# Down projections of both FFNs in blocks of 1024 columns, with seven products for 7 of their 21 pairs of k-tiles

## The chip, the cores and the metric

The kernel runs on one core of one Trainium2 chip. The metric is device microseconds of one execution, median of a few. The core's engines are named as in the profile: PE (TensorE matmul), PEld (its weight loads), DVE (VectorE), ACT (ScalarE), POOL (GpSimd) and SP (SyncE, which issues the loads).

## The reference

One layer of a streaming encoder on 256 tokens of width 2048, all in float32: a half-step SwiGLU FFN, two parallel token mixers, cross-attention into 256 memory tokens and a second half-step FFN, each between a norm ahead and a norm behind, added to the residual x. The change lies in the two FFNs:

```
def swiglu(h, w_gate, w_up, w_down):
    return (jax.nn.silu(h @ w_gate) * (h @ w_up)) @ w_down
...
h = rmsnorm(x, n_ffn1_pre[l])
x = x + 0.5 * rmsnorm(swiglu(h, w_ffn1_gate[l], w_ffn1_up[l], w_ffn1_down[l]), n_ffn1_post[l])
```

D_FF is 5504, so that w_down is 5504 x 2048: 43 k-tiles of 128 rows by 2048 columns.

## The kernel before

Tokens lie in two tiles of 128. All weights are streamed once from HBM, most of them in raw tiles of 128 x 1024 float32 (512 KB). The host has laid them out so that each is one contiguous piece.

**A weight tile's way.** `weights` (L289 to L326) takes one of four raw buffers (`wraw`), loads it from SP's queue (L310), and splits it in two fp32r parts: ScalarE casts it to `whi` (L318), VectorE subtracts, `wlo = wraw - whi` (L319). `whi` and `wlo` hold three slots each. They are used in turn, and the counter `turn` goes on from one linear to the next. The raw buffer is free after the split, the slot when TensorE has multiplied with it.

**The product.** Every product is three matmuls: high part by high part, high by low, low by high. In the down projections (`lin_tok_steps`, L395 to L453; the matmuls are L410 to L412) tokens are stationary and 512 weight columns move, into one PSUM bank for each token tile. A raw tile holds two k-tiles of 512 columns, hence 12 matmuls (2 k-tiles, 2 token tiles, 3 parts). A column block c of 512 columns goes over all 43 k-tiles, and there are four of them. The gate and up projections have their matmuls in L374 and L378.

**An FFN** (`ffn`, L649 to L717) runs gate and up for 256 hidden columns at a time. The evacuations L655 to L668 make silu(gate) x up and split it to `mh` and `ml` (L501, L502; hidden k-tile by tokens), the stationary operands of the down projection. `post_norm` (L602 to L647) runs the four column blocks of the down projection. It squares each result for the norm (L496), multiplies it by the gain into `y` (L637), and in column block 3 makes the updates X += y x rstd (L620). The next norm's transposes are woven into column block 3 (`Passage`, L84 to L176). It also spills X to DRAM (`xsp`, L122) in the FFN ahead of the mixers.

**X**, the residual, is a tile of SBUF. In FFN1 it is loaded from the input in four DMAs of 512 KB during gate and up (L1644). It stays in SBUF through FFN2.

**Order.** Each engine has one instruction stream. A scheduler at build time orders the streams by priority: instructions as written, casts and splits 100 places earlier (`ahead`). A matmul sequence under `manual_schedule` keeps its order on PE. SP's loads stand in the order in which the raw tiles are made and wait for a free buffer.

## Time and profile before

| | |
|---|---|
| median of 3 executions | 2205.06 us (2204.56 to 2208.41) |
| the profiled execution's own time | 2203.17 us |
| its span, first to last instruction | 2201.4 us |
| PE / PEld / DVE / ACT / POOL busy | 2175.5 / 1943.7 / 1460.5 / 1140.5 / 105.8 us |
| mean granted clock of TensorE | 0.998 |
| HBM read and written | 436.51 MB, 10.49 MB |

Times inside an execution are read against the span: the profiled execution lasts 1.8 us longer than the span, and the median shown is 1.9 us above the profiled execution. FFN1's down projection lies at about 459 to 682 us of the span, FFN2's at about 1968 to 2190. In a row of the profile the name before "<-" is what is written and the names behind it are what is read. For a matmul, the name before the comma is the moving operand and the one behind it is the stationary operand.

### The profile page before, as it was taken

The numbers are of one execution on the slowest core, as the hardware profiler recorded it, in microseconds if no ns is written. First come the engines' busy times: TensorE is split into PE (matmuls) and PEld (weight loads), VectorE is DVE, ScalarE is ACT, GpSimd is POOL, SyncE is SP. The second block draws the span as 40 slices with busy tenths as digits, with TensorE's granted clock in tenths as the row PEclk, the third lists the DMA queues.
The fourth block names the chain that finished last, engine by engine and source line by source line (L and its number), as shares of the span: only waits on it lengthen the run. The fifth ranks groups of instructions, "written<-read, shape, count | busy, mean of one in ns | idle before, by whom it ended". The sixth has DMA issues, their size and how long they took to land.

```text
span 2201.4 us, 35059 instructions
## 1 busy us (share of the span) xinstructions
PE 2175.5 (99%) x13664; PEld 1943.7 (88%) x13664; DVE 1460.5 (66%) x2118; ACT 1140.5 (52%) x1706; POOL 105.8 (5%) x177
## 2 busy tenths in 40 slices
PE   9999999999999999999999999999999999999998
PEld 8999999988888889988778889988999999998887
DVE  7666666654457677778778766657766666664444
ACT  7555555544446555664444556446555555554443
POOL 0000000000000100101342000000000000000000
PEclk9999999999999999999999999999999999999999
DMA  7666666666666664555867765555666666666664
GB/s 262 221 210 200 201 201 202 201 213 206 208 210 209 219 209 148 186 173 191 253 201 249 272 206 193 172 176 177 201 201 201 201 201 201 201 209 206 209 204 157
DMA packets 130631, 449.30 MB, mean 204 GB/s; under 512 B 16161, under 2 KB 17697, under 8 KB 130209
## 3 DMA queue, kind: packets, MB, share of 16 engines
q1 hardware_dynamic: 122832, 429.84, 60.6%
q0 software_dynamic: 6768, 16.79, 2.5%
q8 instruction: 107, 1.75, 0.3%
q10 hardware_dynamic: 864, 0.44, 0.1%
q14 instruction: 60, 0.48, 0.1%
HBM read 436.51 MB, written 10.49 MB: 203 GB/s over the span
## 4 chain that ended last, share of the span: by engine, by line
PE 89%; DVE 6%; ACT 2%; issue 2%; DMA 1%; POOL 0%; DVEq 0%; ACTq 0%; POOLq 0%
PE mm L374 32%; PE mm L378 16%; PE mm L410 12%; PE mm L412 12%; PE mm L411 12%; DVE wlo L319 2%; ACT whi L318 1%; DVE tm L1214 0%; PE tr L514 0%; DMA wraw<-in_w_uq 0%; DVE X L620 0%; PE xo L1616 0%; DVE TT L1217 0%; DMA vsh<-vp 0%; PE xsc L1605 0%
## 5 line engine op out<-in xcount | busy, mean ns | idle before, releaser
L319 DVE TENSOR_TENSOR wlo<-wraw,whi 128x1024 fp32r<-128x1024 f32 (+3 forms) x792 | 954.3, 1207 | 618.5 <-ACT whi L318 606.2
L318 ACT CAST whi<-wraw 128x1024 fp32r<-128x1024 f32 (+3 forms) x792 | 818.4, 1034 | 785.3 <-PE mm L412 407.2
L374 PE MATMUL mm<-hT,whi 128*128 128x512 f32 x3280 | 1078.3, 384 | 0.6 <-ACT whi L318 0.6
L378 PE MATMUL mm<-hT,wlo 128*128 128x256 f32 x3280 | 879.9, 274 | 0.6 <-DVE wlo L319 0.6
L374 PEld LDWEIGHTS mm<-hT,whi 128*128 128x128 f32 x3280 | 614.0, 189 | 81.5 <-ACT whi L318 1.1
L378 PEld LDWEIGHTS mm<-hT,wlo 128*128 128x128 f32 x3280 | 630.0, 192 | 6.7 <-DVE wlo L319 1.0
L412 PE MATMUL mm<-whi,ml 128*128 128x512 f32 x680 | 257.8, 379 | 0.0
L410 PE MATMUL mm<-whi,mh 128*128 128x512 f32 x680 | 257.7, 379 | 0.0
L411 PE MATMUL mm<-wlo,mh 128*128 128x512 f32 x680 | 257.7, 379 | 0.0
L410 PE MATMUL mm<-whi,hT 128*128 128x512 f32 (+2 forms) x512 | 182.5, 357 | 0.9 <-DVE gt L1401 0.7
L411 PE MATMUL mm<-wlo,hT 128*128 128x512 f32 (+2 forms) x512 | 179.4, 350 | 1.7 <-DVE wlo L319 1.6
L412 PE MATMUL mm<-whi,hT 128*128 128x512 f32 (+2 forms) x512 | 178.3, 349 | 0.3 <-DVE hT L505 0.3
L411 PEld LDWEIGHTS mm<-wlo,mh 128*128 128x128 f32 x680 | 128.5, 189 | 18.3
L410 PEld LDWEIGHTS mm<-whi,mh 128*128 128x128 f32 x680 | 128.5, 189 | 18.2
L412 PEld LDWEIGHTS mm<-whi,ml 128*128 128x128 f32 x680 | 128.5, 189 | 18.2
L386 ACT COPY half<-mm 128x256 f32<-128x256 f32 x206 | 75.4, 367 | 115.4 <-PE mm L374 115.4
L387 DVE TENSOR_TENSOR half<-half,mm 128x256 f32<-128x256 f32 x206 | 86.0, 418 | 39.8 <-ACT half L386 39.7
L411 PEld LDWEIGHTS mm<-wlo,hT 128*128 128x128 f32 x512 | 97.2, 190 | 13.7 <-DVE wlo L319 4.9
L410 PEld LDWEIGHTS mm<-whi,hT 128*128 128x128 f32 x512 | 97.1, 190 | 12.6 <-DVE gt L1401 1.1
L412 PEld LDWEIGHTS mm<-whi,hT 128*128 128x128 f32 x512 | 97.1, 190 | 10.2 <-DVE hT L505 1.2
L469 POOL TENSOR_TENSOR rstd<-rstd,mhalf 128x1 f32<-128x1 f32 x22 | 15.2, 696 | 1697.7 <-DVE rstd L467 1697.7
L410 PE MATMUL mm<-whi,mT 128*128 128x512 f32 x128 | 48.7, 380 | 0.0
(312 smaller groups left out, 1760.6 us busy)
## 6 DMA issues: line engine op xcount, KB each, us to landing
wraw<-in_w_ffn_up SPq DMA_DIRECT2D x171, 512.0 KB, 3.8
wraw<-in_w_ffn_gate SPq DMA_DIRECT2D x170, 512.0 KB, 3.8
wraw<-in_w_ffn_down SPq DMA_DIRECT2D x168, 512.0 KB, 4.2
wraw<-in_w_in SPq DMA_DIRECT2D x124, 512.0 KB, 3.9
wraw<-in_w_o SPq DMA_DIRECT2D x32, 512.0 KB, 3.6
wraw<-in_w_ckv SPq DMA_DIRECT2D x32, 512.0 KB, 3.8
wraw<-in_w_oa SPq DMA_DIRECT2D x16, 512.0 KB, 3.5
wraw<-in_w_ob SPq DMA_DIRECT2D x16, 512.0 KB, 4.7
```

Source lines behind the costliest of these rows:

```text
L318: cast = self.last_cast = nc.scalar.copy(out=hi[:, e], in_=raw[:, e])
L319: self.last_split = nc.vector.tensor_sub(out=lo[:, e], in0=raw[:, e], in1=hi[:, e].bitcast(F32))
L374: both = lambda: nc.tensor.matmul(ps[j], hi[:, s], self.woven(x[:, k]), start=(k == 0), stop=(k == nk - 1))
L378: nc.tensor.matmul(ps[j][:, 0, :], lo[:, s], self.woven(x[:, k, 0]), start=False, stop=False)
L386: nc.scalar.copy(out=tokens, in_=low)
L387: nc.vector.tensor_add(tokens, tokens, high)
L410: nc.tensor.matmul(ps[t], part(xh, t, k), hi, start=(k == first), stop=False)
L411: nc.tensor.matmul(ps[t], part(xh, t, k), lo, start=False, stop=False)
L412: self.last_mm = nc.tensor.matmul(ps[t], part(xl, t, k), hi, start=False, stop=(k == last))
L469: nc.gpsimd.tensor_tensor(out=r, in0=r, in1=self.mhalf, op=ALU.pow)
```

## The change

The down projection is worked in two blocks of 1024 columns. Of its 43 k-tiles the first 30 are *wide*: a raw tile is one k-tile of 1024 columns. The other 13 are *narrow* as before. `_wide_order` gives the order of the 30: three single k-tiles, then seven times a pair of k-tiles and two singles (one behind the last pair).

A single is 2 token tiles x 2 column halves x 3 = 12 matmuls. A pair of k-tiles, two token tiles and two column halves are a product of 2 x 2 blocks by 2 x 2 blocks. Plainly this takes eight block products; by Strassen's scheme it takes seven, each of three matmuls. Products that belong to one result alone go into its own PSUM bank (`own`), where the singles add too, and the four others into four `shared` banks, over all seven pairs.

The sums of blocks that the scheme needs are made

- on the weight side by four in-place adds of 512 columns on VectorE per pair (L543 to L546), each sum then cast and split by `cut` (cast L510, split L511): w11 with 512 columns, w21|w22, e1|e3 and e4|e2 with 1024 each;
- on the token side by four sums per pair in the evacuation of gate and up (`left`, L488 to L491), kept with their splits in `S`;
- on the result side by `fix_wide` (L566 to L574), once per block: a ScalarE copy and eight VectorE additions on PSUM, with a scratch tile `part` that takes one of the four raw buffers.

`cut` uses six slots: the three of `whi` and `wlo`, and three in `room`, the space of the tile `hT` that is free then. It starts with the first slot in each block. The narrow k-tiles use the ring of three as before (L335 is now the load and L344 the split there). Those of the block's second half begin (k-tiles 30 to 35), then `fix_wide` is issued, then the first half is finished (30 to 42) and evacuated, then the second (36 to 42).

To make room, `y` is kept in two halves, `S` and X share a place, and X is loaded only behind the narrow tiles of column block 2: four DMAs of 512 KB, from the input in FFN1 and from `xsp` in FFN2. The cross-attention writes X to `xsp` for that, eight DMAs of 256 KB. The host lays w_down out in the new order.

```diff
+SPAIRS = range(2, 9)
+WIDE, EARLY = 30, 36
+def _wide_order():
+    rest = [k for k in range(WIDE) if k // 2 not in SPAIRS]
+    out, rest = rest[:3], rest[3:]
+    for i in SPAIRS:
+        out.append((2 * i, 2 * i + 1))
+        out, rest = out + rest[:2], rest[2:]
+    assert not rest
+    return out
...
+    def left(self, g0, g1, mh, ml, k, sh, sl):
+        nc = self.nc
+        d = self.tmp.tile([P, 512], F32, tag="junk", name="sums").rearrange("p (a t) -> p a t", a=4)
+        nc.vector.tensor_sub(d[:, 0], g0[:, P:], g1[:, P:])
+        nc.vector.tensor_sub(d[:, 1], d[:, 0], g0[:, :P])
+        nc.vector.tensor_sub(d[:, 2], g0[:, :P], g0[:, P:])
+        nc.vector.tensor_add(d[:, 3], g1[:, :P], d[:, 1])
+        self.split(g1, mh[:, k + 1, :], ml[:, k + 1, :])
+        self.split(d[:, 0], mh[:, k, P:], ml[:, k, P:])
+        self.split(d[:, 1:], sh, sl)
...
+    def lin_wide(self, w, b, mh, ml, sums, ring, banks):
+        nc = self.nc
+        own, shared = banks
+        seen, turn = set(), [0]
+        last = _wide_order()[-1]
+        def cut(raw):
+            n = raw.shape[-1]
+            hi, lo = (x[:, :n] for x in ring[turn[0] % len(ring)])
+            turn[0] += 1
+            with self.ahead(self.lead):
+                self.last_cast = nc.scalar.copy(out=hi, in_=raw)
+                self.last_split = nc.vector.tensor_sub(out=lo, in0=raw, in1=hi.bitcast(F32))
+            return [(self.paired(hi[:, i : i + 512]), self.paired(lo[:, i : i + 512])) for i in range(0, n, 512)]
+        def product(bank, x, wt, stop=False):
+            (xh, xl), (hi, lo) = x, wt
+            start = id(bank) not in seen
+            seen.add(id(bank))
+            nc.tensor.matmul(bank, xh, hi, start=start, stop=False)
+            nc.tensor.matmul(bank, xh, lo, start=False, stop=False)
+            nc.tensor.matmul(bank, xl, hi, start=False, stop=stop)
+        def load():
+            raw = self.wraw.tile([P, WT], F32, tag="wraw", name="wraw")
+            o = P * WT * (b * KF + self.wide_at)
+            nc.sync.dma_start(out=raw, in_=w[o : o + P * WT].rearrange("(p x) -> p x", p=P))
+            self.wide_at += 1
+            return raw
+        at = lambda k, t: tuple(x[:, k, t * P : (t + 1) * P] for x in (mh, ml))
+        self.wide_at = 0
+        for item in _wide_order():
+            if isinstance(item, int):
+                halves = cut(load())
+                for t in range(NT):
+                    for h in range(2):
+                        product(own[t][h], at(item, t), halves[h], item == last)
+                continue
+            k0, k1 = item
+            ra, rb = load(), load()
+            a0, a1, b0, b1 = ra[:, :512], ra[:, 512:], rb[:, :512], rb[:, 512:]
+            (w11,), (w21, w22) = cut(a0), cut(rb)
+            with self.ahead(self.lead):
+                nc.vector.tensor_add(a0, a0, a1)
+                nc.vector.tensor_add(a1, a1, b1)
+                nc.vector.tensor_add(b1, a0, b1)
+                nc.vector.tensor_add(b0, b1, b0)
+            (e1, e3), (e4, e2) = cut(ra), cut(rb)
+            s2, s3, s4 = sums(k0 // 2 - SPAIRS[0])
+            end = k0 // 2 == SPAIRS[-1]
+            product(shared[0], at(k0, 0), w11, end)
+            product(own[0][0], at(k1, 0), w21)
+            product(own[0][1], s4, w22)
+            product(shared[1], at(k0, 1), e1, end)
+            product(shared[2], s3, e3, end)
+            product(shared[3], s2, e2, end)
+            product(own[1][0], at(k1, 1), e4)
+    def fix_wide(self, banks, part):
+        nc = self.nc
+        own, (p1, p5, p7, p6) = banks
+        u, v = part[:, :512], part[:, 512:]
+        add, sub = nc.vector.tensor_add, nc.vector.tensor_sub
+        with self.ahead(3 * self.lead):
+            nc.scalar.copy(out=u, in_=p1)
+            add(own[0][0], own[0][0], u)
+            add(u, p6, u)
+            sub(v, p5, u)
+            add(u, p7, u)
+            add(own[1][0], own[1][0], u)
+            add(own[0][1], own[0][1], v)
+            sub(v, v, p7)
+            add(own[1][1], own[1][1], v)
...
+            room = self.hpool.tile([P, KD * 2 * T], F32R, tag="hT", name="room", bufs=1)
+            slots = [(x[:, a : a + WT], z[:, d : d + WT]) for x, z, d0 in (
+                (self.whi, self.wlo, 0), (room, room, RING * SLOT)) for a in range(0, RING * SLOT, SLOT) for d in (a + d0,)]
+            banks = {}
+            def narrow(c, ks, ev, *args):
+                base = c // 2 * KF * P * WT + (WIDE * WT + c % 2 * (KF - WIDE) * 512) * P
+                self.lin_tok(
+                    wd, KF, 0, 512, mh, ml, ev, *args, 0, [banks[c // 2][0][t][c % 2] for t in range(NT)],
+                    (ks, lambda k: base + (k - WIDE) * P * 512))
+            def lin(c, ev, passage):
+                b = c // 2
+                if c % 2:
+                    narrow(c, range(EARLY, KF, 2), ev, (7 if passage else SKEW) * (c == 3), passage)
+                    return
+                make = lambda pool, tag: [pool.tile([P, 512], F32, tag=tag, name="mm") for _ in range(2)]
+                one = [make(self.pst, "tr"), make(self.pss, "sm")]
+                two = [make(self.psm, "mm"), make(self.psm, "mm")]
+                own, shared = (two, one) if b else (one, two)
+                banks[b] = [list(x) for x in zip(*own)], [x for p in shared for x in p]
+                with self.tc.manual_schedule(engines={mybir.EngineType.PE}):
+                    self.lin_wide(wd, b, mh, ml, lambda n: [(x[:, 0], x[:, 1]) for x in (sums(n)[:, i] for i in range(3))],
+                                  slots, banks[b])
+                    narrow(c + 1, range(WIDE, EARLY, 2), None, 0, None)
+                    self.fix_wide(banks[b], self.wraw.tile([P, WT], F32, tag="wraw", name="part"))
+                    narrow(c, range(WIDE, KF, 2), ev, 0, None)
+                if b:
+                    self.X = self.hpool.tile([P, NT, D], F32, tag="big", bufs=1, name="X")
+                    for i in range(4):
+                        t, s = i // 2, slice(i % 2 * 1024, (i % 2 + 1) * 1024)
+                        self.after(nc.sync.dma_start(
+                            out=self.X[:, t, s], in_=residual[t * P : (t + 1) * P, s]), self.last_split)
+            return self.post_norm(lin, post, True, *after)
...
-        self.X = self.hpool.tile([P, NT, D], F32, tag="big", name="X")
...
-                    if c0 <= 256 * 5:
-                        feed[1](c0 // 256 - 2)
...
-                a["n_x_post"], False, "n_ffn2_pre")
+                a["n_x_post"], False, "n_ffn2_pre", None, xsp)
```

PE, FFN1's first pair behind the three singles (`mm` is any PSUM bank; `room` and `whi`, `wlo` are slots of weights; `S` holds token sums). The last four of its seven products:

```order
L518 MATMUL mm<-room,mh 128x512
L519 MATMUL mm<-room,mh 128x512
L520 MATMUL mm<-room,ml 128x512
L518 MATMUL mm<-room,S 128x512
L519 MATMUL mm<-room,S 128x512
L520 MATMUL mm<-room,S 128x512
L518 MATMUL mm<-whi,S 128x512
L519 MATMUL mm<-wlo,S 128x512
L520 MATMUL mm<-whi,S 128x512
L518 MATMUL mm<-whi,mh 128x512
L519 MATMUL mm<-wlo,mh 128x512
L520 MATMUL mm<-whi,ml 128x512
```

A pair is 21 rows of this kind; two k-tiles by 1024 columns were 24 rows of L410 to L412.

DVE, inside FFN1's down projection. Before, a column block's tiles follow each other:

```order
L319 TENSOR_TENSOR wlo<-wraw,whi 128x1024 x17
L319 TENSOR_TENSOR wlo<-wraw,whi 128x512
L319 TENSOR_TENSOR wlo<-wraw,whi 128x1024 x2
L637 TENSOR_TENSOR y<-mm,g 128x512
L319 TENSOR_TENSOR wlo<-wraw,whi 128x1024
L637 TENSOR_TENSOR y<-mm,g 128x512
```

Of the change, the last group of block 0 and its end, where the narrow tiles (L344) begin:

```order
L511 TENSOR_TENSOR room<-wraw,room 128x512
L543 TENSOR_TENSOR wraw<-wraw 128x512
L544 TENSOR_TENSOR wraw<-wraw 128x512
L511 TENSOR_TENSOR room<-wraw,room 128x1024 x2
L545 TENSOR_TENSOR wraw<-wraw 128x512
L546 TENSOR_TENSOR wraw<-wraw 128x512
L511 TENSOR_TENSOR wlo<-wraw,whi 128x1024 x2
L344 TENSOR_TENSOR wlo<-wraw,whi 128x1024
L567 TENSOR_TENSOR mm<-mm,part 128x512
L344 TENSOR_TENSOR wlo<-wraw,whi 128x1024
L568 TENSOR_TENSOR part<-mm,part 128x512
L569 TENSOR_TENSOR part<-mm,part 128x512
```

Between the splits stand the sums of a pair, and between the first narrow splits the corrections. The first split of a narrow tile stands ahead of the first correction.

SP, the end of FFN1's down projection and the start of the next linear. Before:

```order
L310 DMA wraw<-in_w_ffn_down 128x1024 x14
L310 DMA wraw<-in_w_ffn_down 128x512
L310 DMA wraw<-in_w_in 128x1024 x5
L122 DMA xsp<-X 128x512 x2
```

And now:

```order
L335 DMA wraw<-in_w_ffn_down 128x1024 x3
L335 DMA wraw<-in_w_ffn_down 128x512
L877 DMA X<-in_x 128x1024 x4
L335 DMA wraw<-in_w_in 128x1024 x4
L148 DMA xsp<-X 128x512
```

The four loads of X stand behind the last tile of w_down and ahead of the first of w_in; they stood among the loads of gate and up before.

More of the change, by code (lines that the diff above doesn't have):

```diff
@@ L402, in lin_tok_steps @@
             self.extra = {extra: passage.slots[0], extra + 2: passage.slots[1]}
-        ps = [self.psm.tile([P, n], F32, tag="mm", name="mm") for _ in range(NT)]
+        begun = ps is not None
+        if not begun:
+            ps = [self.psm.tile([P, n], F32, tag="mm", name="mm") for _ in range(NT)]
         def part(x, t, k):
@@ L409, in step @@
             hi, lo = self.paired(hi), self.paired(lo)
-            nc.tensor.matmul(ps[t], part(xh, t, k), hi, start=(k == first), stop=False)
-            nc.tensor.matmul(ps[t], part(xh, t, k), lo, start=False, stop=False)
-            self.last_mm = nc.tensor.matmul(ps[t], part(xl, t, k), hi, start=False, stop=(k == last))
+            more = {"skip_group_check": True} if begun else {}
+            nc.tensor.matmul(ps[t], part(xh, t, k), hi, start=(k == first and not begun), stop=False, **more)
+            nc.tensor.matmul(ps[t], part(xh, t, k), lo, start=False, stop=False, **more)
+            self.last_mm = nc.tensor.matmul(ps[t], part(xl, t, k), hi, start=False, stop=(k == last), **more)
         held = []
-        for k, hi, lo in self.weights(w, nk, c0, n):
+        for k, hi, lo in self.weights(w, nk, c0, n, at=at):
             if k < before:
@@ L668, in ev_up @@
                     nc.vector.tensor_mul(gate[j], ps, gate[j])
-                    self.split(gate[j], mh[:, k, :], ml[:, k, :])
+                    if k // 2 not in SPAIRS:
+                        self.split(gate[j], mh[:, k, :], ml[:, k, :])
+                    elif j == 0:
+                        self.split(gate[j][:, :P], mh[:, k, :P], ml[:, k, :P])
+                    else:
+                        v = sums(k // 2 - SPAIRS[0])
+                        self.left(gate[0], gate[1], mh, ml, k - 1, v[:, :, 0], v[:, :, 1])
                 return ev_gate, ev_up
```

101 lines of the change are left out of this document (60 added, 41 removed).

## The prediction

> **What bounds the kernel now.** I read the busy times and the chain of waits first, then the sums of the two stretches in which the down projections run, then single rows there.
>
> ```profile
> span 2201.4 us, 35059 instructions
> PE 2175.5 (99%) x13664; PEld 1943.7 (88%) x13664; DVE 1460.5 (66%) x2118; ACT 1140.5 (52%) x1706; POOL 105.8 (5%) x177
> PE 89%; DVE 6%; ACT 2%; issue 2%; DMA 1%; POOL 0%; DVEq 0%; ACTq 0%; POOLq 0%
> ...
> 460.00:682.00 222.00, 222.00 (x1031) 194.28 (x1031) 112.18 (x106) 95.10 (x106) 0.55 (x1) 1.00 0.67 210
> 1968.00:2190.00 222.00, 222.00 (x1030) 194.43 (x1029) 108.59 (x103) 92.88 (x102) 0.55 (x1) 1.00 0.64 196
> ```
>
> The last two rows are windows (length; then busy time and instructions of PE, PEld, DVE, ACT and POOL; granted clock; DMA share; GB/s). In both, TensorE is busy from end to end at clock 1.00, VectorE half of the time. TensorE alone sets the time there, so removing matmuls pays in full as long as what feeds it keeps up. 222.00 / 1031 = 0.2153 us is the distance of two matmuls; the busy time of one (below) is longer because matmuls overlap. The same from single rows of the timeline (start, duration):
>
> ```profile
> 588.04 0.38 PE L412 MATMUL mm<-whi,ml 128*128 128x512 f32 x1
> 588.68 0.38 PE L412 MATMUL mm<-whi,ml 128*128 128x512 f32 x1
> 589.10 1.05 ACT L318 CAST whi<-wraw 128x1024 fp32r<-128x1024 f32 x1 [1.54 <-PE mm L412]
> 590.18 1.23 DVE L319 TENSOR_TENSOR wlo<-wraw,whi 128x1024 fp32r<-128x1024 f32 x1 [1.37 <-ACT whi L318]
> 591.69 1.05 ACT L318 CAST whi<-wraw 128x1024 fp32r<-128x1024 f32 x1 [1.54 <-PE mm L412]
> 593.22 0.38 PE L412 MATMUL mm<-whi,ml 128*128 128x512 f32 x1
> ```
>
> The first and the last PE row are 24 matmuls apart: (593.22 - 588.04) / 24 = 0.2158 us, which I use. A tile of 12 matmuls takes 2.59 us, the distance of the casts. A cast waits for TensorE to leave its slot: it starts 0.04 us behind the end of the slot's last matmul (588.68 + 0.38), 0.2 after the next matmul's turn. The split starts 0.03 us after the cast's end. Both are done long before the tile is used, as the three slots run ahead.
>
> **What is saved.** A pair of k-tiles by seven products of three matmuls takes 21 matmuls where it took 24. 7 pairs x 2 blocks x 2 FFNs = 28 pairs save 84 matmuls, and 84 x 0.2158 = **18.1 us**. The busy time of a row is the wrong price:
>
> ```profile
> L412 PE MATMUL mm<-whi,ml 128*128 128x512 f32 x680 | 257.8, 379 | 0.0
> ```
>
> 84 x 0.379 would be 31.8 us, but the 379 ns of neighbours overlap.
>
> **What VectorE and ScalarE get for it.** A steady group is now a pair and two single k-tiles: 21 + 24 = 45 matmuls, 9.71 us of TensorE. Prices of the new work:
>
> ```profile
> L319 DVE TENSOR_TENSOR wlo<-wraw,whi 128x1024 fp32r<-128x1024 f32 x761 | 931.4, 1225 | 612.3 <-ACT whi L318 600.1 <-PE xpt L1610 0.5
> L318 ACT CAST whi<-wraw 128x1024 fp32r<-128x1024 f32 x761 | 797.6, 1048 | 776.3 <-PE mm L412 402.9 <-PE mm L374 164.2 <-issue 118.4
> L319 DVE TENSOR_TENSOR wlo<-wraw,whi 128x512 fp32r<-128x512 f32 x11 | 7.5, 685 | 1.0 <-ACT whi L318 1.0
> L318 ACT CAST whi<-wraw 128x512 fp32r<-128x512 f32 x11 | 6.7, 617 | 1.8 <-PE mm L412 1.7
> L1541 DVE TENSOR_TENSOR t<-t,ya 128x512 f32<-128x512 f32 x8 | 5.5, 686 | 0.0
> L637 DVE TENSOR_TENSOR y<-mm,g 128x512 f32<-128x512 f32 x32 | 21.9, 684 | 1.4 <-ACT junk L496 1.4
> ...
> 665.62 1.22 DVE L319 TENSOR_TENSOR hT<-wraw,hT 128x1024 fp32r<-128x1024 f32 x1 [0.39 <-ACT hT L318]
> 666.76 1.22 DVE L319 TENSOR_TENSOR wlo<-wraw,whi 128x1024 fp32r<-128x1024 f32 x1
> ```
>
> Two splits that follow each other start 1.14 us apart, 0.08 less than the duration; so a 512-column add is 0.61 behind unrelated work and 0.69 + 0.03 = 0.72 where it needs the one before. VectorE per group: five splits of 1024 (w21|w22, e1|e3, e4|e2, two singles) 5.70, the 512 one 0.61, four adds about 2.6, together 8.9 us of 9.71, or 92%, where it had 50%. ScalarE: 5 x 1.05 + 0.62 = 5.9. Neither is over the 9.71, so throughput costs nothing; what remains is latency through the buffers.
>
> **The loop through the buffers.** Four raw buffers, four loads of 512 KB per group. Loads already wait for a buffer:
>
> ```profile
> SPq L310 <- DVE wlo L319: 1205.2, 533, 6.9
> wraw<-in_w_ffn_down SPq DMA_DIRECT2D x168, 512.0 KB, 4.2
> ...
> wraw<-in_w_ffn_down SPq DMA_DIRECT2D x13, 512.0 KB, 3.4
> ...
> wraw<-in_w_in SPq DMA_DIRECT2D x1, 512.0 KB, 3.5
> ...
> wraw<-in_w_ob SPq DMA_DIRECT2D x16, 512.0 KB, 4.7
> ```
>
> (Issue to landing, KB and us: the page's median of 4.2; a stretch at 472 to 508 us with 3.4; one load at 914 that came alone behind another, 3.5; the slowest group, 4.7.) In the new order the second raw tile of a pair goes into the buffer that the group's first single leaves, and this single's split stands behind the pair's work on VectorE. Around that loop: load L; hand-over 0.03; cast w21|w22 1.05; 0.03; its split 1.14; split e1|e3 1.14; adds L545 and L546 0.72 + 0.61; the single's split 1.23; 0.03: L + 5.98 us. Against 9.71 it binds if L is over 3.7. I take L = 3.5: no other load is issued in the 2.5 us ahead of it and few bytes are in flight (the 3.4 and 3.5 rows). Then 9.5 < 9.71 and the loop costs 0. At 4.2 each group is 0.5 us late, six groups on end per block less the lead of 2 us, about 1.7 per block, 7 us in four blocks; at 4.7, 4 x (6 x 1.0 - 2) = 16 us.
>
> The Trainium skill, "DMA: Bandwidth & Descriptors", section "Anatomy of one DMA", gives for another issuing path 2.0 us plus the bytes at 436 GB/s, by estimate 3.2 us for this tile. By that the loop would be 9.2 us and the sum the same; no row here shows 512 KB under 3.4, so the rule is the kinder end.
>
> **Where slots clash.** The wide block always begins at slot 0 of its six and ends with k-tile 29 in slot 1, while the ring of three of the other linears goes on from where it stood. Followed through the tables: FFN1's block 0 and FFN2's block 1 begin when slot 0 still holds the tile TensorE has just multiplied. The first cast can then start only behind that tile's last matmul: 0.2 + 1.05 + 0.03 + 1.23 - 0.2 (one matmul needs no split) = 2.3 us of idle TensorE that nothing covers, twice, **4.7 us**. In the same two blocks k-tile 30 wants slot 1, which k-tile 29 still holds: 2.4 each, since its split can stand behind a correcting add; FFN1's block 1 half a microsecond, FFN2's block 0 nothing: **5.3 us**. If loads take 4.2 us these last become 3.7, 3.7 and 3.0, together 10.4. The bounds: nothing, if each cast finds a free slot; and load, cast and split in a row (3.5 + 1.05 + 1.23, some 6 us) at both ends of the four blocks, 46 us. I take the value near the low end, as only the clashes named have no free slot, and the raw tiles are there.
>
> **The rest.** Eight corrections per block on VectorE (L567 to L574, 0.69 each by the two add rows, 5.5 us, behind one ScalarE copy) are issued beside three narrow tiles, 7.8 us of TensorE; with the three splits VectorE has 8.9 us there, 1.1 too many, and makes it up in the ten narrow tiles behind, where it has 1.14 us of work per 2.59: 0. Uncovered they would cost 4 x 5.5 = 22 us. For the first group of the two blocks that begin without a clash I put 0.6 together. The sums on the token side (L488 to L491 and the smaller splits) lie in the column blocks of gate and up, some 21 us each:
>
> ```profile
> 453.89 0.42 DVE L502 TENSOR_TENSOR ml<-sg,mh 128x256 fp32r<-128x256 f32 x1
> ...
> 420.00:441.50 21.50, 21.50 (x133) 19.78 (x132) 14.90 (x22) 11.21 (x17) 0.00 (x0) 1.00 0.61 197
> ```
>
> Splits of 1024, 512 and 256 take 1.22, 0.69 and 0.42, so 128 columns about 0.29 and 384 about 0.55: two splits of 256 (0.84) become one of 256, two of 128, one of 384 and four sums of 128, 2.7 us, 1.9 more. VectorE goes from 14.9 to 16.8 of 21.5, 78%, hidden by the three slots of lead: 0. Without that cover it would be 14 pairs x 1.9 = 27 us. X late: four DMAs of 512 KB queue on SP ahead of the first tiles of the next stage in FFN1 (and ahead of the last w_down tiles in FFN2). X is needed only by the first update in column block 3, some 11 us after issue, and four transfers at 210 GB/s last 10: 0 to 1.6 in FFN2, I put 0.5. The eight spills of 256 KB in the cross-attention lie on a queue whose windows leave a third of the DMA time: 0 to 1. Without cover, 2 MB at 210 GB/s is 10 us each.
>
> **Sum.** -18.1 + 0 (loop) + 4.7 + 5.3 + 0.6 + 0.5 + 0.4 (spill) = -6.6 us against the profiled execution of 2203.2 us (span 2201.4 and 1.8 around it), 2196.6. The median shown is 2205.06, 1.9 above the profiled one; on its scale **2198.5 us**.
>
> **Rivals.**
> 1. *The loading loop decides, slower.* If w_down tiles land in 4.2 us, the page's median, the loop is 10.2 > 9.71: -18.1 + 7 + 4.7 + 10.4 + 1.5 = +5.5, 2210.6; at 4.7 some +14, 2219. It decides from L = 3.7 and turns the sign near 3.9. For: the median row. Against: the 3.4 and 3.5 rows at a like distance of issues, and that 216 GB/s (2 MB per 9.71 us) is hardly above the 210 of today.
> 2. *It ends level.* L between 3.7 and 4.0 costs 2 to 5 us in the loop and 2 more at the hand-overs: 2201 to 2207. For: nothing in the rows parts 3.5 from 3.9 in a new rhythm.
> 3. *The change gives its full 18.* If the slots are free in time or the clash costs only a cast, the loss is under 3 us: 2187 to 2190. Against: cast and split are in order on engines whose rows show no shorter form.
> 4. *The clock falls in the new gaps.* A TensorE that waits 3.7 us (rival 1's hand-overs) could be granted a lower clock behind it: at half speed for as long again it loses 1.8 us, with three such gaps 5.5, so 2216. For and against: no row above holds a gap of this size, so the profile of before cannot say. The Trainium skill, "TensorE: Matmul & The Clock Gate", section "What's actually happening", has the clock fall to half after an idle window of about 3.4 us; by it the gaps of my forecast, 2.4 us, change nothing, and those of rival 1 may. The row of the windows, 1.00 throughout, bears on neither.
>
> **How the numbers follow.** About 0.2%, 4.4 us, can be told from no change: same is 2200.6 to 2209.5. Forecast 0.45 with its own range 2192 to 2203 (0.36 of it faster, 0.09 same); rival 1 0.24 (0.20 slower, 0.04 same); rival 2 0.18 (0.15 same, 0.02 slower, 0.01 faster); rival 3 0.10, faster; rival 4 0.03, slower. Faster 0.47, same 0.28, slower 0.25. The range runs from 2190, which leaves out most of rival 3, to 2214, which leaves out the far end of rival 1 and rival 4.
>
> **What would show it.** TensorE with 84 fewer matmuls at the same 0.216 us, and in the two wide stretches PE idle only at block starts (about 2.3, cast and split named as releasers, L518 and L519) and at k-tile 30 (L410, L411). If rival 1 is right, each group shows an idle of L518 or L519 on `room` tiles, behind a cast that waited for a DMA, and w_down loads of 4 us or more. If rival 3 is right, no gap over 1 us stands there. An idle PE in gate and up, or at L620's X, would mean that covers I counted as whole are not. I am wrong altogether if VectorE, at 92% of a group, is what TensorE waits for without any load being late.

## The result: slower by 1.2%

| | before | changed |
|---|---|---|
| median | 2205.51 us (2204.56 to 2208.41, 4 runs) | 2232.9 us (2226.64 to 2234.2, 4 runs) |
| ratio | | 1.0116, 95% interval 1.0095 to 1.0138 |
| profiled execution, span | 2203.17 us, 2201.4 us | 2234.20 us, 2232.4 us |

The forecast was 2198.5 us, in a range from 2190 to 2214. The time lies outside it, and the sign is wrong. The two spans by stage (windows of the trace: length; then busy time and instructions of PE, PEld, DVE, ACT and POOL; granted clock; DMA share; GB/s), first before, then the changed kernel. The stages are gate and up of FFN1, its down projection, everything up to FFN2's down projection, and that:

```profile
0.00:459.40 459.40, 457.21 (x2774) 419.81 (x2775) 320.48 (x459) 249.88 (x374) 2.79 (x9) 1.00 0.66 212
459.40:682.70 223.30, 223.30 (x1038) 195.39 (x1037) 112.85 (x109) 95.91 (x108) 0.55 (x1) 1.00 0.67 211
682.70:1967.90 1285.20, 1272.04 (x8823) 1133.60 (x8822) 912.10 (x1442) 700.43 (x1120) 99.15 (x164) 1.00 0.62 202
1967.90:2190.80 222.90, 222.90 (x1033) 194.88 (x1031) 109.49 (x104) 92.88 (x102) 0.55 (x1) 1.00 0.63 195
```

```profile
0.00:460.10 460.10, 456.50 (x2774) 418.11 (x2774) 331.35 (x501) 253.68 (x388) 2.80 (x9) 1.00 0.64 208
460.10:696.60 236.50, 223.84 (x994) 189.76 (x994) 180.69 (x204) 116.43 (x136) 0.55 (x1) 0.98 0.61 203
696.60:1987.40 1290.80, 1274.22 (x8824) 1133.22 (x8823) 924.45 (x1488) 704.99 (x1135) 99.60 (x164) 1.00 0.63 203
1987.40:2222.00 234.60, 222.21 (x991) 188.81 (x989) 179.06 (x204) 114.08 (x132) 0.55 (x1) 0.98 0.59 195
```

The down projections have 42 matmuls fewer each and yet last 13.2 and 11.7 us longer: 24.9 of the 31.0 us between the spans. TensorE idles in them for 12.7 and 12.4 us, where it was busy throughout, and its granted clock is 0.98 instead of 1.00. The stage between is 5.6 us longer, gate and up 0.7.

**What TensorE waited for** (engine and line, what ended the wait; us in all, times, longest; the whole execution), before and now:

```profile
PE mm L411 <- DVE wlo L319: 2.2, 4, 0.9
```

```profile
PE mm L439 <- DVE wlo L344: 11.2, 13, 2.3
PE mm L519 <- DVE wlo L511: 9.1, 18, 1.0
PE mm L518 <- ACT whi L510: 5.0, 4, 3.4
PE mm L438 <- ACT whi L343: 3.9, 4, 1.1
```

L519 is the wait inside the pairs, mostly for e4|e2's split, 18 times up to 1 us. L518 is mostly the block starts. L438 is the step to the narrow tiles, and so are 6.3 us of L439; its other 4.9 lie in the stage between, where L411 had the 2.2 before. The rows of the step in FFN1's block 0:

```profile
539.68 0.38 PE L520 MATMUL mm<-whi,ml 128*128 128x512 f32 x1
541.19 0.48 PE L438 MATMUL mm<-whi,mh 128*128 128x512 f32 x1 [1.13 <-ACT whi L343]
543.92 0.48 PE L439 MATMUL mm<-wlo,mh 128*128 128x512 f32 x1 [2.24 <-DVE wlo L344]
544.24 0.50 PE L440 MATMUL mm<-whi,ml 128*128 128x512 f32 x1
544.53 0.63 PE L438 MATMUL mm<-whi,mh 128*128 128x512 f32 x1
544.96 0.63 PE L439 MATMUL mm<-wlo,mh 128*128 128x512 f32 x1
```

Between 539.68 and 543.92 lie 3.8 us more than two matmuls' distance. From 544.5 on matmuls follow each other at 0.43 us instead of 0.216, until 547.9. The granted clock of that stretch, and of the one behind it, in windows:

```profile
543.90:547.90 4.00, 3.98 (x11) 3.17 (x12) 1.27 (x2) 0.00 (x0) 0.00 (x0) 0.57 0.49 157
548.50:552.50 4.00, 4.00 (x20) 3.50 (x19) 1.77 (x2) 1.88 (x2) 0.00 (x0) 1.00 0.17 54
```

Eleven matmuls in 4 us at clock 0.57, then twenty at 1.00. This half clock comes behind five gaps of this execution. From the starts of consecutive matmuls, each distance over 0.3 us less 0.216 (and the run of 0.43 us distances likewise), the two down projections lose:

| | forecast | measured |
|---|---|---|
| matmuls saved | -18.1 | -18.1 |
| block starts (FFN1 block 0, FFN2 block 1) | 4.7 | 2.4 + 4.6 = 7.0 |
| step to the narrow tiles (three blocks) | 5.3 | 3.8 + 3.1 + 3.9 = 10.8 |
| inside the pairs, four blocks | 0 | 2.7 + 5.2 + 4.8 + 1.8 = 14.5 |
| half clock behind the five gaps | 0 | 1.7 + 1.7 + 1.7 + 1.7 + 2.7 = 9.5 |
| others (forecast: first groups of two blocks; measured: last tiles of FFN2) | 0.6 | 1.3 |
| down projections, sum | -7.5 | +25.0 |

**The loads.** The four loads of a group in FFN1's block 0 (timeline of SP's queue; then the DMA view of 501 to 522 us, two groups: GB/s in 40 equal slices, and the median from issue to landing; last, what the casts into `room` waited for in the whole execution):

```profile
501.66 4.55 SPq L525 DMA_DIRECT2D wraw<-in_w_ffn_down  x4
...
GB/s 0 0 0 133 320 406 180 164 211 304 297 304 304 281 351 351 273 117 0 0 0 0 0 148 328 406 187 117 179 367 281 289 296 265 297 390 304 117 8 31
...
wraw<-in_w_ffn_down SPq DMA_DIRECT2D x8, 512.0 KB, 4.7
...
ACT room L510 <- DMA wraw<-in_w_ffn_down: 71.9, 49, 3.3
```

All four are issued within 4.6 us, then none for 6, and for the five slices of 0 nothing moves. By place in the group, a block's means are 3.7 to 4.1 us for the pair's first tile, 4.3 to 4.7 for its second, 4.8 to 5.1 for the singles.

### The profile page after: what moved, and what is told of

Read it like the earlier page. It is cut to its first block, busy times and chain, and to the rows that moved or that the text cites. A ratio compares the mean times of both kernels' runs of the same rounds, so it can differ in the third digit from the quotient of the medians.

```text
span 2232.4 us, 35351 instructions
## 1 busy us (share of the span) xinstructions
PE 2176.8 (98%) x13580; PEld 1929.9 (86%) x13580; DVE 1621.1 (73%) x2402; ACT 1190.6 (53%) x1794; POOL 106.2 (5%) x177
## 4 chain that ended last, share of the span: by engine, by line
PE 68%; DVE 11%; DMA 9%; issue 7%; ACT 4%; POOL 1%; SPq 0%; ACTq 0%; DVEq 0%; POOLq 0%
PE mm L399 30%; PE mm L403 15%; DMA wraw<-in_w_ffn_down 7%; PE mm L439 6%; PE mm L438 6%; PE mm L440 6%; DVE wlo L344 3%; DVE room L511 3%; ACT whi L343 2%; DVE wlo L511 1%; ACT room L510 1%; DVE wraw L545 1%; PE mm L519 1%; PE mm L520 1%; DMA squares<-in_xT 1%
## 5 line engine op out<-in xcount | busy, mean ns | idle before, releaser
L344 DVE TENSOR_TENSOR wlo<-wraw,whi 128x1024 fp32r<-128x1024 f32 (+3 forms) x672 | 807.1, 1203 | 433.1 <-ACT whi L343 424.6
L343 ACT CAST whi<-wraw 128x1024 fp32r<-128x1024 f32 (+3 forms) x672 | 691.5, 1030 | 594.1 <-PE mm L440 240.6
L439 PE MATMUL mm<-wlo,hT 128*128 128x512 f32 (+2 forms) x512 | 180.3, 352 | 4.1 <-DVE wlo L344 3.8
L438 PE MATMUL mm<-whi,hT 128*128 128x512 f32 (+2 forms) x512 | 182.5, 357 | 0.9 <-DVE gt L1564 0.7
L411 ACT COPY half<-mm 128x256 f32<-128x256 f32 x206 | 75.8, 369 | 116.2 <-PE mm L399 116.2
L510 ACT CAST whi<-wraw 128x1024 fp32r<-128x1024 f32 x92 | 94.2, 1046 | 66.0 <-DVE wraw L546 38.5
L511 DVE TENSOR_TENSOR wlo<-wraw,whi 128x1024 fp32r<-128x1024 f32 x92 | 110.4, 1222 | 16.9 <-ACT whi L510 16.1
L510 ACT CAST room<-wraw 128x1024 fp32r<-128x1024 f32 (+1 forms) x84 | 74.0, 903 | 84.9 <-DMA wraw<-in_w_ffn_down 71.9
L412 DVE TENSOR_TENSOR half<-half,mm 128x256 f32<-128x256 f32 x206 | 86.1, 418 | 39.9 <-ACT half L411 39.8
L439 PEld LDWEIGHTS mm<-wlo,hT 128*128 128x128 f32 x512 | 97.1, 190 | 19.1 <-DVE wlo L344 10.5
L518 PE MATMUL mm<-whi,mh 128*128 128x512 f32 x284 | 109.1, 384 | 4.5 <-ACT whi L510 4.5
L519 PE MATMUL mm<-wlo,mh 128*128 128x512 f32 x284 | 109.3, 385 | 1.6 <-DVE wlo L511 1.6
L520 PE MATMUL mm<-whi,ml 128*128 128x512 f32 x284 | 108.9, 383 | 0.0
L438 PEld LDWEIGHTS mm<-whi,hT 128*128 128x128 f32 x512 | 97.1, 190 | 12.6 <-DVE gt L1564 1.1
L511 DVE TENSOR_TENSOR room<-wraw,room 128x1024 fp32r<-128x1024 f32 (+1 forms) x84 | 86.1, 1045 | 17.1 <-ACT room L510 16.5
```

Source lines behind the costliest of these rows:

```text
L343: cast = self.last_cast = nc.scalar.copy(out=hi[:, e], in_=raw[:, e])
L344: self.last_split = nc.vector.tensor_sub(out=lo[:, e], in0=raw[:, e], in1=hi[:, e].bitcast(F32))
L438: nc.tensor.matmul(ps[t], part(xh, t, k), hi, start=(k == first and not begun), stop=False, **more)
L439: nc.tensor.matmul(ps[t], part(xh, t, k), lo, start=False, stop=False, **more)
L510: self.last_cast = nc.scalar.copy(out=hi, in_=raw)
L511: self.last_split = nc.vector.tensor_sub(out=lo, in0=raw, in1=hi.bitcast(F32))
```

## The experiments

**Slots (e1).** The first theory to test was that starts and steps are clashes of slots. The wide block begins at the slot that is due next, and the ring behind it goes on at the slot free longest:

```diff
+            ring = lambda: slots[self.turn : RING] + slots[: self.turn] + slots[RING:]
...
-                                  slots, banks[b])
+                                  ring(), banks[b])
+                    self.turn = (self.turn + 2) % RING
```

> Only the slots are turned: the wide block begins at the slot of the ring that is due next, and the ring behind it goes on at the slot that has been free longest. Work, loads and sums stay as they are. Theory (slot clash at block starts and at the step to the narrow tiles, and a clock that falls behind these gaps): the five gaps of 2.4, 3.8, 3.1, 4.6 and 3.9 us go, and with them the half clock behind each (9.5 us together); the small stalls at each pair (14 us in all) stay. 2232.9 - 17.8 - 9.5 + some 3 for what stays of late loads = 2208 us (2204 to 2214). Rival (the gaps come from the corrections of fix_wide in VectorE's queue or from late loads): the two starts go, the steps to the narrow tiles stay with their half clock: about 2222 us.

Measured: 2216.58 us (1.0048, 1.0031 to 1.0065), 16 us less than the changed kernel. All five gaps and the half clock behind them are gone from the down projections, the steps with the corrections included, so the rival is out as a cause of its own. But the gain is 9 us short of the sum:

```profile
460.00:684.00 224.00, 217.48 (x992) 185.69 (x991) 179.34 (x204) 115.98 (x135) 0.55 (x1) 1.00 0.66 213
1978.20:2204.60 226.40, 218.04 (x991) 185.81 (x989) 178.61 (x204) 113.91 (x132) 0.55 (x1) 1.00 0.62 202
```

TensorE still idles 6.5 and 8.4 us. The stalls at the pairs, counted as above, grew from 14.5 to 23, which is about what the sum lacks. As I read it, a gap at a block's start had given loads and splits a lead, and without it the first pairs stall too.

**The single earlier (e2), and both (e3).** The loop through the buffers was to be shortened by casting and splitting the first single behind a pair ahead of the pair's last sums:

```diff
             (w11,), (w21, w22) = cut(a0, 3), cut(rb, 4)
...
+            e1, e3 = cut(ra, 5)
+            ready[order[n + 1]] = cut(load(), turn[0])
+            with self.ahead(self.lead):
                 nc.vector.tensor_add(b1, a0, b1)
                 nc.vector.tensor_add(b0, b1, b0)
-            (e1, e3), (e4, e2) = cut(ra), cut(rb)
+            e4, e2 = cut(rb, 1 - turn[0])
```

> Only the order on ScalarE and VectorE inside a group is changed: the first single behind a pair is cast and split before the pair's last sums, so that its raw buffer, into which the next pair's second tile goes, comes free earlier; to allow it the slots of this single and of e4|e2 change places from pair to pair. Same work, same four buffers. Theory (latency of the loop load, cast, splits, sums, single's split): L + 5.98 becomes about L + 4.8, with L of 4.4 us 9.2 < 9.71; the stalls at the pairs (2.7, 5.2, 4.8 and 1.8 us per block) go, the gaps at starts and steps stay: 2232.9 - 13 = 2220 us (2216 to 2225). Rival (VectorE is simply too full at 92 per cent of a group): the same 2233 us, within 3.

> Both edits together, the turned slots and the early single. Theory: the losses add, so both gains do: 2232.9 - 25 - 13 = 2195 us (2190 to 2202), faster than the kernel before (2205.5). Rival (VectorE too full, or gaps from the corrections): 2210 or more.

Measured: 2232.7 us (1.0126, 1.0110 to 1.0141) and 2223.36 us (1.0084, 1.0069 to 1.0099). No gain alone, and 7 us worse than e1 together. By the words on record this speaks for a VectorE that is too full. The trace of e2 shows another reason (SP's queue, then VectorE, at 517 to 528 us):

```profile
517.14 0.33 SPq L524 DMA_DIRECT2D wraw<-in_w_ffn_down  x1
...
522.66 1.23 DVE L510 TENSOR_TENSOR wlo<-wraw,whi 128x1024 fp32r<-128x1024 f32 x1 [0.39 <-ACT whi L509]
523.80 1.22 DVE L510 TENSOR_TENSOR room<-wraw,room 128x1024 fp32r<-128x1024 f32 x1
524.93 0.68 DVE L550 TENSOR_TENSOR wraw<-wraw 128x512 f32<-128x512 f32 x1
526.78 2.36 DVE L510 TENSOR_TENSOR wlo<-wraw,whi 128x1024 fp32r<-128x1024 f32 x2 [1.17 <-ACT whi L509]
...
528.04 0.33 SPq L524 DMA_DIRECT2D wraw<-in_w_ffn_down  x1
```

The single now takes the buffer of the pair's second tile. Its load (4.3 us), cast and split stand ahead of e1|e3's split, the last sum L550, e4|e2's cast and split, and that split frees the buffer for the next single's load: 528.04 - 517.14 = 10.9 us a turn, over 9.71 again. VectorE idles 0.39 and 1.17 us in it. The edit had put one loop in the place of another, and it could not tell the theories apart.

**Busy gaps (e4).** This run tests whether the slow matmuls come from TensorE's idleness. Fourteen matmuls of zeros go ahead of k-tile 30, at the three steps that had gaps:

```diff
+                    for _ in range(0 if passage_in and not b else 14):
+                        nc.tensor.matmul(banks[b][0][0][1], zero, S[1][:, :2].rearrange("p a b x -> p (a b x)"),
+                                         start=False, stop=False, skip_group_check=True)
                     narrow(c + 1, range(WIDE, EARLY, 2), None, 0, None)
```

> The changed kernel with 14 matmuls of zeros (3.0 us) ahead of k-tile 30, added to a result bank, at the three steps to the narrow tiles that had gaps of 3.8, 3.1 and 3.9 us. The gaps' cause stays. Theory (the half clock behind a gap comes from TensorE's idleness): the matmuls fit into the gaps, the clock stays whole there, and the 1.7, 1.7 and 2.7 us lost to it come back: 2232.9 - 6 = 2227 us. Rival (the slow matmuls behind the gaps have another cause, as late operands): the slow stretch stays and the time is 2233 us or more.

Measured: 2222.79 us (1.0084, 1.0069 to 1.0099), 10 us less for 42 more matmuls. The filled gap and the four us behind it:

```profile
539.60:542.60 3.00, 3.00 (x14) 2.45 (x14) 2.68 (x4) 1.20 (x2) 0.00 (x0) 1.00 0.60 182
543.70:547.70 4.00, 4.00 (x19) 3.52 (x20) 1.49 (x3) 1.05 (x1) 0.00 (x0) 1.00 0.47 158
```

Nineteen matmuls at clock 1.00 where there were eleven at 0.57. No slow stretch is left behind any of the three filled steps, so the idleness was its cause; by the count in the changed kernel it had cost 6 us there. The rest of the 10 belongs to other places: the stage between the down projections is 3.4 us shorter in this trace (below), and the half clock behind FFN1's block start (1.7) did not come, though its gap of 2.4 us is still there.

**A fifth raw buffer (e5), and with the turned slots (e6).** The same VectorE work in the same order, and one buffer more:

```diff
-        self.wraw = mk("wraw", 4)
+        self.wraw = mk("wraw", 5)
-        self.gp = mk("gp", 2)
+        self.gp = mk("gp", 1)
-            y = self.tmp.tile([P, T], F32, tag="half", name="half", bufs=2)
+            y = self.tmp.tile([P, T], F32, tag="half", name="half", bufs=1)
-SLOT = WT + 128
+SLOT = WT + 64
```

> The changed kernel with five raw buffers in place of four; room for the fifth comes from a single buffer for the gain tile and for the half sums and from slots that lie 1088 instead of 1152 apart. Order, slots and work stay. Theory (the stalls at the pairs are a loop of load, cast, splits and sums through too few buffers; the second run only put another loop of 10.8 us in place of the first): with a fifth buffer the next pair's second tile no longer waits for the single's split, all the stalls at the pairs (some 14 us) go and the gaps at starts and steps stay: 2232.9 - 13 = 2220 us (2216 to 2225). Rival (VectorE too full at 92 per cent): the stalls stay, 2230 to 2236.

> Five raw buffers and the turned slots of the first run. Theory: the first run's 2216.6 less its stalls at the pairs (15 us in its trace) = 2202 us (2197 to 2207), and if all waits but the late X go about 2195. Rival (VectorE too full): 2214 to 2218.

Measured: 2209.42 us (1.0023, 1.0013 to 1.0033) and **2193.84 us (0.9956, 0.9941 to 0.9971)**. The second beats both kernels, and lies below the 2197 to 2207 that its expectation gave: that sum had put e1's stalls at the pairs at 15 us where the count gives 23. In the window 492 to 554 us, which holds five groups and the step, first the changed kernel, then e6:

```profile
492.00:554.00 62.00, 57.00 (x251) 47.77 (x250) 49.19 (x55) 29.49 (x32) 0.00 (x0) 0.97 0.55 187
```

```profile
492.00:554.00 62.00, 62.00 (x289) 54.30 (x288) 50.76 (x56) 30.58 (x32) 0.00 (x0) 1.00 0.64 209
```

TensorE is busy all the time, with VectorE at 50.8 of 62 us: it was never too full, it came too late. The loads still take 4.5 us at the median, but the casts into `room` wait 25.5 us for them instead of 71.9. A loop with room in it does not mind. e5 alone gained 23 us where 13 were expected: its trace has no stall at a pair but the first ones, of the three steps one is gone and two are shorter (2.45 us each instead of 3.8 and 3.9), and no half clock follows them.

**X in pieces (e7, e8), gain tiles on another queue (e11, e12).** In the changed kernel the four loads of X stand behind all narrow tiles of column block 2. In three runs they stand between them: e7 is e1 with this edit, e8 is e6 with it.

```diff
-                    narrow(c, range(WIDE, KF, 2), ev, 0, None)
...
+                    for i, ks in enumerate((range(30, 34, 2), range(34, 36, 2), range(36, 38, 2), range(38, KF, 2))):
+                        narrow(c, ks, ev if i == 3 else None, 0, None)
+                        if b:
+                            t, s = i // 2, slice(i % 2 * 1024, (i % 2 + 1) * 1024)
+                            self.after(nc.sync.dma_start(
+                                out=self.X[:, t, s], in_=residual[t * P : (t + 1) * P, s]), self.last_split)
```

e11 is e6 with the FFNs' gain tiles issued from GpSimd's queue, where no tile of a weight is ahead of them, and e12 has both edits:

```diff
-            self.after(nc.sync.dma_start(out=g, in_=post[:, s].partition_broadcast(P)), before)
+            self.after((nc.gpsimd if half else nc.sync).dma_start(out=g, in_=post[:, s].partition_broadcast(P)), before)
```

> The first run's turned slots, and X loaded in four pieces between the narrow tiles of column block 2 instead of behind them. Theory (the 2.1 us gap of TensorE at FFN1's first transposes and the 1.7 us of half clock behind it come from X and the w_in tiles queued behind X, which took 9 us to land): both go, 2216.6 - 4 = 2212.5 us. Rival (the pieces only push the last w_down tiles back): the same 2216.6, within 2, with a new gap inside column block 2 or 3.

> All three: five buffers, turned slots, X in pieces. Theory (losses add): e6 less 4, about 2198 us, below the kernel before (2205), with the mixers' own part between 0 and 6 us above before. If every loss were gone it would be 2205 - 18 = 2187; I expect the first pair of each block and the mixers to keep some 8 us. Rival: not under 2205, since with five buffers loads come in larger bunches and the narrow tiles and mixers pay for it.

> e6 with the FFNs' gain tiles loaded from GpSimd's queue instead of SP's. In e6's trace the last gain tile was issued behind the four loads of X and landed 1.7 us after VectorE wanted it, with a TensorE gap of 1.55 us at FFN1's first transposes. Theory: that gap goes, 2193.8 - 1.6 = 2192 us. Rival (the gap is X's own): the same 2193.8, within 2.

> e11 (five buffers, turned slots, gain tiles from GpSimd's queue) with X loaded in four pieces between the narrow tiles of column block 2, as in e7 and e8. In e11's trace the last gain tile, issued when its single buffer came free, landed 6.2 us later because four X loads and three w_in tiles were under way, and VectorE waited 2.5 us for it. Theory (the gain tile is late because of the burst of X): it lands in about 4 us, the TensorE gap of 2.3 us at FFN1's first transposes and the 1.7 us of half clock behind it go: 2195.8 - 3.5 = 2192 us. Rival (with one gain buffer it is late anyway): 2195 to 2197.

Measured: e7 2214.06 us (1.0043, 1.0028 to 1.0058), 2.5 less than e1, in the direction expected, though the intervals overlap; the gap at the first transposes shrank from 2.1 to 0.5 us, as the theory had it, and one of 1.0 appeared in column block 3, as the rival had it. e8 2196.02 (0.9958, 0.9942 to 0.9975), e11 2195.8 (0.9962, 0.9950 to 0.9975), e12 2197.51 (0.9966, 0.9954 to 0.9978): none is better than e6, and the intervals overlap. In all three VectorE waits 2.5 to 2.8 us for a gain tile of FFN1 (1.7 in e6): there is only one buffer for it, the other paid for the fifth raw buffer. VectorE in e12 at the first update of FFN1:

```profile
672.20 0.21 DVE L588 TENSOR_SCALAR rstd<-ss,tot 128x1 f32<-128x1 f32 x1 [1.45 <-ACT junk L617]
675.14 0.69 DVE L758 TENSOR_TENSOR y<-mm,g 128x512 f32<-128x512 f32 x1 [2.72 <-DMA g<-in_n_ffn_post]
```

The gain tile can be issued only when the last column block's evacuation has let go of its buffer, and lands 5.6 us later (6.2 in e11), whether it is loads of X or of w_in that are under way beside it. Here the rival was right, with a time half a microsecond above its range.

**Controls (e9, e10).** e6 without any pair (the 30 wide k-tiles as singles, without the sums and corrections), and the kernel before with e6's memory:

```diff
-SPAIRS = range(2, 9)
+SPAIRS = range(0)
...
-    rest = [k for k in range(WIDE) if k // 2 not in SPAIRS]
...
+    out = list(range(WIDE))
...
-                    self.fix_wide(banks[b], self.wraw.tile([P, WT], F32, tag="wraw", name="part"))
```

> e6 (five buffers, turned slots) with no pair at all: the 30 wide k-tiles are singles, the token sums, the weight sums and the corrections are not there, the product is the plain one. Theory (a pair saves three matmuls at their distance of 0.216 us and, with e6's buffers, costs nothing): 2193.8 + 84 x 0.216 = 2212 us (2209 to 2215), so that the wide form without pairs is some 7 us slower than the kernel before. Rival A (a saved matmul is worth its busy time of 0.379 us): 2226. Rival B (e6 gained by its five buffers and not by its pairs): under 2205.

> The kernel before with the same memory edit as e6: five raw buffers, one gain tile, one half-sum tile, slots 1088 apart; nothing else. Theory (before has no loop that waits for a raw buffer with TensorE idle): no gain, 2204.5 us, within 3, or 1 to 2 more where the gain tile comes late. Rival (the fifth buffer alone explains e6's gain over before): 2194 to 2198.

Measured: 2206.39 us (1.0009, 1.0000 to 1.0018) and 2204.82 us (1.0004, 0.9995 to 1.0013). The fifth buffer alone gives nothing, and neither does the wide form without pairs, so e6's gain is the pairs'. But e9 was expected at 2212 (2209 to 2215): the pairs are worth 12.6 us, not 18.1. FFN2's down projection in e9, then in e6:

```profile
1970.20:2193.00 222.80, 222.80 (x1033) 194.82 (x1031) 108.60 (x104) 92.12 (x102) 0.55 (x1) 1.00 0.63 203
```

```profile
1966.60:2181.50 214.90, 213.99 (x991) 186.64 (x989) 177.30 (x204) 113.70 (x132) 0.55 (x1) 1.00 0.65 211
```

42 matmuls less, 7.9 us, and TensorE idles 0.9 at the first pair: 8.8 us, or 0.21 a matmul. There the price is right. FFN1's is 8.5 us shorter, and 8.9 without the gaps of both (3.7 us in e6, 3.3 in e9 with a half clock at its first transposes). What is missing lies mostly in the stage between, 4.5 us longer in e6 than in e9. The prediction had nothing there, and of the runs' expectations only e8's names the mixers.

## Why the prediction was wrong

**Right.** The price of a matmul, 0.2158 us and not the 0.379 of its busy time (e9 against e6). The places of loss at the starts and steps, and that FFN2's block 0 has no gap at its step. That the loop has L + 5.98 us and binds over 3.7: with the measured second load of 4.4 it is 10.4, and the groups of FFN1's block 0 follow each other at 10.3 to 10.75 us (the pairs' first loads at 480.61, 491.36, 501.66, 512.12 and 522.52). The cover of `left` held: gate and up grew by 0.7 us. Half right is X: its cover is not whole, but the gap of 1.7 us stands at FFN1's first transposes, where the forecast had nothing; the 0 to 1.6 were put down for FFN2.

**The step that failed first: "I take L = 3.5".** It gave 0 for a loop that cost 14.5. The row of 3.5 us was one load behind another in an idle stretch. I had counted the loads ahead of the second tile and not those behind it: the group's four loads come within 4.6 us, as their buffers come free in a row when VectorE is through, and share the transfer. The page's median of 4.2 was nearer, as rival 1 had it (7 us there, at 4.7 it had 16). The 7 is a slip: by the sum beside it, 4 x (6 x 0.47 - 2), it is 3. With the measured 4.4 that sum gives 8, so the lead of 2 us per block was not there in full either; single stalls of 1.5 us in FFN1's block 1 were not followed further. The rhythm of issues is itself made by the loop, so a load's time could not be taken from a stretch with even spacing.

**The second: "2.4 each" for the steps and 2.3 for the starts.** At the steps 3.8, 3.1 and 3.9 us, of the size that rival 1 gave for late loads (3.7, 3.7 and 3.0). The rows of ScalarE and VectorE at 539 us show what I left out:

```profile
539.10 2.04 ACT L343 CAST whi<-wraw 128x1024 fp32r<-128x1024 f32 x2 [0.90 <-DMA wraw<-in_w_ffn_down]
...
541.32 0.68 DVE L568 TENSOR_TENSOR part<-mm,part 128x512 f32<-128x512 f32 x1
542.04 0.69 DVE L569 TENSOR_TENSOR part<-mm,part 128x512 f32<-128x512 f32 x1
542.65 1.22 DVE L344 TENSOR_TENSOR wlo<-wraw,whi 128x1024 fp32r<-128x1024 f32 x1
```

The cast that TensorE needs is the second of the two at 539.10. The first, of a later tile, waits 0.9 us for its load and stands in front. That cost nothing here: the slot came free at 540.06, with the end of the last wide matmul, and the needed cast began at 540.10. But the needed split, ready at 541.17, began at 542.65, behind two corrections: 1.5 us, which is the surplus over the 2.4 (that had room for 0.1). At FFN2's block 1 the step shows the same 1.5. At FFN1's block 1, forecast at 0.5, the needed cast (657.72) does stand behind one that waited for its load until 656.76, and its split 0.8 us behind a correction. At the start of FFN2's block 1 the slot is free at 2099.17, but the first single's cast (2101.42) stands behind one that waits for its load until 2100.90, and the start costs 4.6. The order of these instructions was to be read from the changed kernel. I had priced the clash as if the engines were free when the slot was.

**The third: the clock at nothing.** Rival 4 had it, at 3 in 100, and only behind gaps of 3.7 us. It fell behind all five gaps, from 2.4 us on, and cost 9.5. The Trainium skill, "TensorE: Matmul & The Clock Gate", section "What's actually happening", has the clock fall after an idle window of about 3.4 us, from which I took gaps of 2.4 to change nothing. The trace agrees with the length and not with the idleness: in the 3.41 us ahead of the fall at 544.37 TensorE was busy for 0.93 (rows in the last section); the measurement decides. The same section of the Trainium skill lets the window run freely, not from the start of a gap. There the traces agree (last section).

**The range** went wrong because I treated these as rivals of which one would come true. They are one chain: bunched loads make the loop, the late loads lengthen the gaps, and the gaps cost the clock. Rival 1's 2210.6 and the 9.5 of the clock make 2220; the 7 us that the loop cost beyond rival 1's and 2 at the starts bring it to 2229; the stage between, 5.6 us longer, brings it to 2235, 2 over the measured 2232.9.

**Open.** Between the first `gr` and the first `po<-S,ar` matmul, in the mixers, nothing was changed: VectorE has the same instructions in the same order. Windows of that stretch before, in the changed kernel, in e6 and in e9, and what a 512 KB DMA from GpSimd's queue took in before and in the changed kernel; last, a stretch inside the same one of e1:

```profile
988.16:1078.38 90.22, 90.14 (x1030) 77.14 (x1030) 72.89 (x124) 41.71 (x51) 13.61 (x23) 1.00 0.68 216
...
LT<-ld POOLq DMA_DIRECT2D x1, 512.0 KB, 3.6
```

```profile
1002.75:1096.11 93.36, 92.56 (x1031) 76.68 (x1030) 72.88 (x124) 41.56 (x51) 13.65 (x23) 1.00 0.66 208
...
LT<-ld POOLq DMA_DIRECT2D x1, 512.0 KB, 5.3
```

```profile
981.33:1075.63 94.30, 92.60 (x1031) 76.68 (x1030) 72.86 (x124) 41.60 (x51) 13.64 (x23) 1.00 0.64 206
```

```profile
988.36:1078.89 90.53, 90.32 (x1030) 77.05 (x1029) 72.88 (x124) 41.70 (x51) 13.63 (x23) 1.00 0.67 215
```

```profile
1079.64:1083.05 3.41, 3.41 (x9) 2.69 (x9) 0.85 (x2) 1.39 (x3) 0.00 (x0) 0.50 0.86 272
```

Without pairs the stretch takes 90.2 and 90.5 us, and 91.5 in e10; with them 93.4 and 94.3, but 91.2 in e4, and 96.5 in e1, of which some 1.7 is the half clock of the last row. So the two kinds overlap, with one trace of each kernel. The busy times are the same; VectorE waits longer for that DMA's result (2.7 us in the changed kernel, 2.8 in e6, 0.4 in e9). That it meets weight loads in another phase is argued, not shown: no run moved it. Of the 5.6 us that the stage between is longer in the changed kernel, this stretch is 3.1 and the late X some 1.5.

## What to carry to other kernels

Take a load's time for a loop through few buffers from the rhythm that the new order will have: where the buffers come free in a row, the loads are issued in a row and each takes longer, and an engine that is busy 80% of the time can still be late each time around. Where a ring of slots meets another one, read what stands ahead of the first cast and the first split in each engine's order; three lines that let the rings go on from each other were worth 16 us here. A saved matmul is worth its distance to the next, but only when the price of feeding the rest has been paid: here one more buffer and the slots turned the change from 1.2% slower to 0.4% faster.

## What was not expected of the hardware

The clock fell behind gaps much shorter than I had thought, and not each time. The traces' records of the granted clock show what decides. In all 14 traces together it falls to 0.50 in 21 places ahead of the end. Eighteen of these stretches last 3.41 us and three last 6.83, and within an execution their starts lie whole multiples of 3.413 us apart: in the changed kernel 462.45, 544.37, 660.42, 2104.26 and 2182.76, which are steps of 24, 34, 423 and 23 times that. So the clock is set anew on a fixed grid and not at the start or end of a gap. Three neighbouring windows of that grid at the step of FFN1's block 0:

```profile
540.96:544.37 3.41, 0.93 (x3) 0.61 (x4) 3.38 (x5) 0.18 (x1) 0.00 (x0) 1.00 0.68 246
544.37:547.78 3.41, 3.41 (x10) 2.66 (x9) 0.80 (x2) 0.00 (x0) 0.00 (x0) 0.50 0.50 154
547.78:551.19 3.41, 3.41 (x17) 2.98 (x17) 1.23 (x1) 1.36 (x2) 0.00 (x0) 1.00 0.00 0
```

TensorE idles 2.48 us in the first, the second runs at half clock, the third at the whole one. Counted by the profile's rows over all windows of all traces that begin at full clock: the 16 with at least 1.9 us without a matmul were all followed by the half clock, of the 22 with 1.4 to 1.9 us five were, and of the others none. A gap of 2.4 us therefore costs 2.4 or about 4, as it lies within one window or across two. That would fit the wider spread of the changed kernel's runs (7.6 us against 3.9); it was not tested by a run that moves a gap against the grid.
